# Softmax division moved from the probabilities to the result of P V, in the attention blocks of a hybrid decoder kernel

## The chip, the cores and the metric

The kernel runs on one core of one Trainium2 chip. It is measured in device microseconds (us) from start to end of one execution; less is better. The core has a matrix engine (PE, with its weight loads as PEld), a vector engine (DVE), a scalar engine (ACT), GpSimd (POOL) and a queue engine (SP). Each runs its own list of instructions in order and waits for the others by semaphores. PE writes to PSUM, which is cut into banks; DVE and ACT read PSUM and the on-chip memory SBUF.

## What is computed

The reference is a decoder trunk of two layers over 512 tokens of width 1024, in float32. Each layer has three mixers side by side (sparse attention, a diagonal state space "S5", a chunked state space "SSD"), an output projection, and an MLP of width 4096. Only the attention matters here, cut to its core:

```python
def attend(args):                              # one block of 128 queries
    ...
    _, sel = lax.top_k(score, topk)            # 128 keys for each query
    ...
    logits = jnp.where(valid[:, :, None, None, :], logits, -jnp.inf)
    p = jax.nn.softmax(logits, axis=-1).astype(v_sel.dtype)
    o = jnp.einsum('bqgrk,bqkgd->bqgrd', p, v_sel)
    return o.reshape(b, Q_BLOCK, ATTN_WIDTH)
```

There are 8 heads of width 64: 2 key/value groups g with 4 heads r each. There are 4 query blocks per layer.

## The kernel before

Each layer is written as several streams of work (projections, index scores, top-k, attention, S5, SSD, output projection), as Python generators that `merge` steps in turn by the costs that they yield (`pace`, `start`); the instructions then get their places on each engine from a priority list (`prio`) and from when buffers come free. So a change in one stream also shifts where the instructions of others stand. PSUM has two pools of four banks, "m" and "a"; the plan of each layer says which pool a tile comes from.

`attend` handles one query block b, with (b + 1) x 128 keys. For each group g and head r: PE makes the logits `lg` (L1033, in `head_dot`), DVE applies the top-k mask and takes the row's extreme in one pass (L1085, tile `pe`), and ACT does exp in place, with the row sum into `sm` (L1086; the tile's name in the trace is `psum`). After the four heads of a group, DVE takes the reciprocal of the sums (L1089). Then the four tiles of probabilities are multiplied by it: head 0 on ACT (L1093, from the plan's `norm_act`), heads 1 to 3 on DVE (L1095). For each 128 keys, PE transposes the four tiles of a group (L1101, tile `pTp`), ACT copies them to SBUF (L1103, `pT`), and PE multiplies with the values (L1106, `po`; group 0 to PSUM partitions 0 to 63, group 1 to 64 to 127). At the end each of four 128x128 slices of `po` is split in a high part `mh` (ACT, L1110) and a low part `ml` (DVE, L1111), which feed the output projection (`pm`, L436 to L438, result added to x by DVE at L1341).

Work that stands between, on the same engines: top-k (MAX and MATCH_REPLACE, L1064 and L1065, DVE), the SSD mixer (`cv`, `CT` L836, `dec` L874 on DVE; `arow`, `ssds` L871, `ssdy` L885 and L887, `st` on PE), the S5 mixer (`X` L714 on DVE; `s5y`, `glu` on PE), and the split of the next block's queries (`hhl` L1021 on DVE, then `hTp` on PE).

Of the kernel before, what the change touches and what calls it, by code (L numbers as in the profile page):

```python
# [10 lines left out]
F32 = mybir.dt.float32  # L11
F32R = mybir.dt.float32r
I32 = mybir.dt.int32
AF = mybir.ActivationFunctionType
ALU = mybir.AluOpType
# [3 lines left out]
P = 128  # L19
# [26 lines left out]
    "top": ((1, 2, 3),),  # L46
    "out": (("att",), ("s5", "ssd")),
    "serial": "no",
    "norm_act": (),
    "tab_dve": (),  # L50
    "pace": {"w": 1.0, "key": 1.0, "idx": 1.0, "top": 1.0, "q": 1.0, "att": 1.0, "s5": 1.0, "ssd": 1.0, "out": 1.0,
             "tab": 1.0},
    "start": {"tab": 0.0, "key": 0.0, "top": 0.0, "att": 0.0, "s5": 0.0, "ssd": 0.0, "out": 0.0},
    "prio": {},
# [3 lines left out]
}  # L58
# [3 lines left out]
        "top": ((2, 1), (3,)),  # L62
        "out": (("s5",), ("att",), ("ssd",)),
        "serial": "no",
        "norm_act": (0,),
        "tab_dve": ("B1", "C2"),
        "pace": {"w": 0.29, "key": 2.007, "idx": 0.686, "top": 0.061, "q": 3.616, "att": 1.702, "s5": 0.084, "ssd": 2.496, "out": 1.504, "tab": 0.3},
        "start": {"tab": 0.5, "key": 5.0, "top": 41.0, "att": 0.0, "s5": 12.0, "ssd": -7.0, "out": 20.0},
        "prio": {"att": 300, "idx": -30, "top": -300, "ssd": 300, "tab": -30, "w": 30, "s5": 30, "out": -30, "q": -300},
        "bank": {"w_kv": "m", "w_qi": "m", "w_q": "m", "w_u5": "m", "w_xa": "a", "w_xb": "m", "w_z": "m", "kT": "a", "hT": "a", "ix": "a", "lg": "a", "pT": "m", "po": "a", "sB": "m", "sst": "a", "sU": "a", "sv": "m", "sy": "m", "st": "m", "sg": "a", "dds": "a", "dseg": "m", "darow": "m", "dT": "a", "ds": "a", "dy": "a", "dst": "a", "dn": "a", "db": "m"},  # L70
    },
    {
        "w_order": ("kv", "xa", "qi", "z", "u5", "q", "xb"),
        "top": ((1,), (2,), (3,)),
        "out": (("s5",), ("att",), ("ssd",)),
        "serial": "no",
        "norm_act": (0,),
        "tab_dve": (),
        "pace": {"w": 0.344, "key": 1.011, "idx": 1.036, "top": 0.873, "q": 3.741, "att": 1.652, "s5": 0.357, "ssd": 1.82, "out": 0.453, "tab": 0.853},
        "start": {"tab": 0.0, "key": 0.0, "top": 15.0, "att": -20.0, "s5": -30.0, "ssd": 3.0, "out": 22.0},  # L80
        "prio": {"tab": -30, "out": -100, "att": 1000, "q": -300, "idx": -30, "s5": 1000, "top": -100},
        "bank": {"w_kv": "m", "w_qi": "m", "w_q": "m", "w_u5": "m", "w_xa": "a", "w_xb": "m", "w_z": "m", "kT": "a", "hT": "a", "ix": "b", "lg": "a", "pT": "a", "po": "a", "sB": "m", "sst": "a", "sU": "m", "sv": "m", "sy": "a", "st": "b", "sg": "a", "dds": "a", "dseg": "m", "darow": "m", "dT": "m", "ds": "m", "dy": "a", "dst": "a", "dn": "a", "db": "m"},
    },
)
WB = (3, 5)
# [115 lines left out]
class Net:  # L201
# [868 lines left out]
    def attend(self, b, qT, K, mask, nrs, ah, al):  # L1070

        nc = self.nc
        v = nc.vector
        nk = (b + 1) * P
        po = self.ps(self.bank["po"], (P, 4, P), name="po")
        es = []
        for g_ in range(2):
            sm = self.s([P, 4], tag="psum", bufs=4)
            for r in range(4):
                p = self.ps(self.bank["lg"], name="lg")[:, :nk]  # L1080
                self.head_dot(p, qT[2 * r + g_], K, g_, nk)
                e = self.g(name="pe")[:, :nk]
                nm = self.s([P, 1], tag="nmax", bufs=8)
                h = 2 * r + g_
                v.tensor_tensor_reduce(e, p, mask, nrs[:, h:h + 1], 3.0e38, ALU.add, ALU.min, nm)  # L1085
                nc.scalar.activation(e, e, AF.Exp, bias=nm, scale=-1.0, accum_out=sm[:, r:r + 1])  # L1086
                es.append(e)
                yield self.pace["att"] * (0.4 + 0.25 * b)
            v.reciprocal(sm, sm)  # L1089
            for r in range(4):  # L1090
                e = es[4 * g_ + r]
                if r in self.plan["norm_act"]:
                    nc.scalar.activation(e, e, AF.Copy, scale=sm[:, r:r + 1])  # L1093
                else:
                    v.tensor_scalar(e, e, sm[:, r:r + 1], None, ALU.mult)  # L1095
        for kb in range(b + 1):
            pts = []
            for g_ in range(2):
                p = self.ps(self.bank["pT"], (P, 4, P), name="pTp")
                for r in range(4):  # L1100
                    nc.tensor.transpose(p[:, r], es[4 * g_ + r][:, kb * P:(kb + 1) * P], self.ident)  # L1101
                pt = self.g([P, 4, P], name="pT")
                nc.scalar.activation(pt, p, AF.Copy)  # L1103
                pts.append(pt)
            for g_ in range(2):
                nc.tensor.matmul(po[g_ * 64:g_ * 64 + 64], self.vt[:, kb, g_], pts[g_], start=kb == 0, stop=kb == b)  # L1106
            yield self.pace["att"] * 2.2
        bs = slice(b * P, (b + 1) * P)
        for r in range(4):
            nc.scalar.activation(ah[r][:, bs], po[:, r], AF.Copy)  # L1110
            v.tensor_tensor(al[r][:, bs], po[:, r], ah[r][:, bs].bitcast(F32), ALU.subtract)  # L1111


    def merge(self, name, streams):
# [409 lines left out]
```

## Time and profile before

| | us |
|---|---|
| median of 3 runs | 1334.06 (1333.53 to 1334.45) |
| the profiled execution, its own time | 1331.74 |
| its span, first to last instruction | 1330.0 |
| PE busy in the span | 1219.8 (92%) |
| DVE busy | 884.2 (66%) |
| ACT busy | 554.9 (42%) |

The granted clock of PE is 0.962 of full on average over the span. In the trace's rows, a start is in us from the span's first instruction, then comes the time that the row spans, the engine, the line, what is written from what, the shape, the number of records, and in brackets the idle time of that engine just before with what ended it. A matmul in full float32 leaves two records.

### The profile page before, as it was taken

Reading aid. Unit: us, or ns where it says so; the run is one execution under the profiler, and the core shown is the slowest. Engines: PE = TensorE matmul, PEld = TensorE weight load, DVE = VectorE, ACT = ScalarE, POOL = GpSimd, SP = SyncE. Lnnn points to the kernel's source line nnn. Section 1 sums busy time; section 2 is a strip of 40 time slices with the busy share of each in tenths; the row PEclk is TensorE's granted clock in tenths of the full one; section 3 lists DMA queues with packets and bytes.
Section 4 is the critical chain, followed back from the end, with each engine's and each line's share of the span. In section 5 each row is a group of like instructions: output and inputs, shape, how many; then the busy total and the mean of one; then the engine's idle time right before and its main releaser. Section 6 shows DMA issues by size and latency. Waiting matters only on the chain. (4 is left out here: it accounts for less than half of the span.)

```text
span 1330.0 us, 16738 instructions
## 1 busy us (share of the span) xinstructions
PE 1219.8 (92%) x5708; PEld 979.4 (74%) x5708; DVE 884.2 (66%) x2024; ACT 554.9 (42%) x1128; POOL 167.1 (13%) x302
## 2 busy tenths in 40 slices
PE   5678967889999999999999978967999999999998
PEld 5657755458888877888887867744788888888886
DVE  7998999857865444454575899996575445444443
ACT  4345543664532432423445535655354233242331
POOL 2494100000696030000000000000000000000000
PEclk9789978899999999999999989978999999999999
DMA  6122220002333323333323332100133333333332
GB/s 197 48 72 64 73 81 22 11 1 71 95 97 103 95 62 118 97 96 96 97 79 82 102 83 58 47 9 17 51 93 95 98 100 96 96 96 99 99 111 80
DMA packets 107430, 105.83 MB, mean 80 GB/s; under 512 B 15184, under 2 KB 99920, under 8 KB 107344
## 3 DMA queue, kind: packets, MB, share of 16 engines
q1 hardware_dynamic: 107344, 104.76, 26.5%
q8 instruction: 45, 0.74, 0.2%
q14 instruction: 41, 0.34, 0.1%
HBM read 100.41 MB, written 3.15 MB: 78 GB/s over the span
## 5 line engine op out<-in xcount | busy, mean ns | idle before, releaser
L172 DVE TENSOR_TENSOR wlo<-wraw,whi 128x512 fp32r<-128x512 f32 (+1 forms) x368 | 260.5, 710 | 285.0 <-ACT whi L171 284.1
L171 ACT ACTIVATE whi<-wraw 128x512 fp32r<-128x512 f32 (+1 forms) x368 | 229.1, 624 | 487.0 <-PE pm L437 343.1
L436 PE MATMUL pm<-xh,whi 128*128 128x512 f32 x640 | 252.4, 395 | 3.9 <-ACT q L1199 3.9
L437 PE MATMUL pm<-xl,whi 128*128 128x512 f32 x640 | 251.5, 393 | 0.0
L438 PE MATMUL pm<-xh,wlo 128*128 128x512 f32 x640 | 250.7, 392 | 0.0
L438 PE MATMUL pm<-uh,wlo 128*128 128x512 f32 x512 | 199.3, 390 | 1.2 <-DVE wlo L172 1.2
L437 PE MATMUL pm<-ul,whi 128*128 128x512 f32 x512 | 199.4, 390 | 0.0
L436 PE MATMUL pm<-uh,whi 128*128 128x512 f32 x512 | 199.4, 389 | 0.0
L436 PEld LDWEIGHTS pm<-xh,whi 128*128 128x128 f32 x640 | 121.0, 189 | 30.5 <-ACT q L1199 4.6
L438 PEld LDWEIGHTS pm<-xh,wlo 128*128 128x128 f32 x640 | 121.1, 189 | 25.4 <-DVE wlo L172 0.2
L437 PEld LDWEIGHTS pm<-xl,whi 128*128 128x128 f32 x640 | 121.1, 189 | 24.4 <-issue 0.2
L438 PEld LDWEIGHTS pm<-uh,wlo 128*128 128x128 f32 x512 | 96.1, 188 | 21.7 <-DVE wlo L172 1.6
L437 PEld LDWEIGHTS pm<-ul,whi 128*128 128x128 f32 x512 | 96.1, 188 | 20.3 <-issue 0.4
L436 PEld LDWEIGHTS pm<-uh,whi 128*128 128x128 f32 x512 | 96.1, 188 | 20.0 <-issue 0.2
L436 PE MATMUL pm<-whi,xh 128*128 128x512 f32 (+1 forms) x176 | 67.8, 388 | 13.8 <-ACT xh L372 11.7
L437 PE MATMUL pm<-wlo,xh 128*128 128x512 f32 (+1 forms) x176 | 66.8, 380 | 4.9 <-DVE wlo L172 4.9
L438 PE MATMUL pm<-whi,xl 128*128 128x512 f32 (+1 forms) x176 | 66.4, 382 | 2.2 <-DVE xl L374 2.2
L1376 DVE TENSOR_TENSOR ul<-ur,uh 128x512 fp32r<-128x512 f32 x64 | 48.4, 757 | 22.5 <-ACT uh L1375 22.4
L1374 DVE SCALAR_TENSOR_TENSOR ur<-pm,ur 128x512 f32<-128x512 f32 x64 | 43.9, 686 | 24.4 <-ACT ur L1371 24.4
L1382 DVE TENSOR_TENSOR sq<-pm,r2b 128x512 f32<-128x512 f32 x64 | 44.2, 690 | 23.1 <-PE pm L438 23.1
L1375 ACT ACTIVATE uh<-ur 128x512 fp32r<-128x512 f32 x64 | 40.0, 625 | 32.4 <-DVE ur L1374 32.4
L436 PE MATMUL pm<-mh,whi 128*128 128x512 f32 x128 | 51.4, 403 | 0.7 <-DVE x L1341 0.7
(343 smaller groups left out, 1859.3 us busy)
## 6 DMA issues: line engine op xcount, KB each, us to landing
wraw<-in_w_up_dram SPq DMA_DIRECT2D x128, 256.0 KB, 2.7
wraw<-in_w_down_dram SPq DMA_DIRECT2D x128, 256.0 KB, 2.7
wraw<-in_w_in_dram SPq DMA_DIRECT2D x64, 256.0 KB, 2.8
wraw<-in_w_out_dram SPq DMA_DIRECT2D x32, 256.0 KB, 2.7
wraw<-in_w_in_dram SPq DMA_DIRECT2D x16, 166.0 KB, 2.3
x<-in_xT_dram SPq DMA_DIRECT2D x8, 256.0 KB, 5.6
out_dram<-x SPq DMA_DIRECT2D x8, 256.0 KB, 2.1
s5bc<-in_s5bc_dram SPq DMA_DIRECT2D x4, 256.0 KB, 4.4
```

Source lines behind the costliest of these rows:

```text
L171: nc.scalar.activation(hi, raw, AF.Copy)
L172: nc.vector.tensor_tensor(lo, raw, hi.bitcast(F32), ALU.subtract)
L436: nc.tensor.matmul(p, lh, rh, start=first, stop=False)
L437: nc.tensor.matmul(p, lh, rl, start=False, stop=False)
L438: nc.tensor.matmul(p, ll, rh, start=False, stop=last)
L1374: v.scalar_tensor_tensor(r, p, 0.0, r, ALU.max, ALU.mult)
L1375: nc.scalar.activation(h, r, AF.Copy)
L1376: v.tensor_tensor(lo, r, h.bitcast(F32), ALU.subtract)
L1382: v.tensor_tensor(t, d[1], rb, ALU.mult)
```

## The change

The probabilities stay undivided. `sm` now holds the sums of both groups, and one reciprocal of 128x8 follows the last exp of the block. Eight small matmuls (`rsb`, after L1091) take a column of reciprocals, repeated to 64 columns, as the stationary operand and the identity as the moving one. This puts the reciprocals of a head along the free axis and the same row on 64 partitions, in the layout of `po`. ACT copies the bank to SBUF (`rn`, after L1093). After P V, DVE multiplies `po` by `rn` in one 128x512 pass (after L1107), and `mh` and `ml` are made from `rn` in SBUF. The scalings and the plan's `norm_act` are gone. `rsb` takes a bank of pool "m" in layer 0 and of "a" in layer 1. For the code around it, a line of the kernel after is the line of before less 3 ahead of the reciprocal, and less 1 to 3 behind it.

```diff
         es = []
+        sm = self.s([P, 2, 4], tag="psum", bufs=2)
         for g_ in range(2):
-            sm = self.s([P, 4], tag="psum", bufs=4)
             for r in range(4):
...
-                nc.scalar.activation(e, e, AF.Exp, bias=nm, scale=-1.0, accum_out=sm[:, r:r + 1])
+                nc.scalar.activation(e, e, AF.Exp, bias=nm, scale=-1.0, accum_out=sm[:, g_, r:r + 1])
                 es.append(e)
                 yield self.pace["att"] * (0.4 + 0.25 * b)
-            v.reciprocal(sm, sm)
-            for r in range(4):
-                e = es[4 * g_ + r]
-                if r in self.plan["norm_act"]:
-                    nc.scalar.activation(e, e, AF.Copy, scale=sm[:, r:r + 1])
-                else:
-                    v.tensor_scalar(e, e, sm[:, r:r + 1], None, ALU.mult)
+        v.reciprocal(sm, sm)
+
+        p = self.ps(self.bank["rsb"], (P, 4, P), name="rsb")
+        for r in range(4):
+            for g_ in range(2):
+                nc.tensor.matmul(p[g_ * 64:g_ * 64 + 64, r], sm[:, g_, r:r + 1].to_broadcast([P, 64]), self.ident, start=True, stop=True)
+        rn = self.g([P, 4, P], name="rn")
+        nc.scalar.activation(rn, p, AF.Copy)
         for kb in range(b + 1):
...
+        v.tensor_tensor(rn, po, rn, ALU.mult)
         for r in range(4):
-            nc.scalar.activation(ah[r][:, bs], po[:, r], AF.Copy)
-            v.tensor_tensor(al[r][:, bs], po[:, r], ah[r][:, bs].bitcast(F32), ALU.subtract)
+            nc.scalar.activation(ah[r][:, bs], rn[:, r], AF.Copy)
+            v.tensor_tensor(al[r][:, bs], rn[:, r], ah[r][:, bs].bitcast(F32), ALU.subtract)
```

Over the whole program PE gets 64 matmuls more, DVE goes from 1882 to 1834 instructions and ACT from 1044 to 1036. The change also moves others.

PE in layer 0, block 2, before, from the last logits: the first four transposes are followed by the first P V matmul of group 0 alone, then by `ssdy`, and group 1's transposes come after that.

```order
L1033 MATMUL lg_2731<-kl_767,hT_2626 128x384
L1101 MATMUL pTp_2743<-cons,pe_2661 128x128
...
L1106 MATMUL po_2656<-pT_2748,vt_119 64x512
L885 MATMUL ssdy_2775<-dec_2650,xd_2690 64x128
L887 MATMUL ssdy_2775<-cs_2728,prev_2637 64x128
...
L1101 MATMUL pTp_2750<-cons,pe_2704 128x128
```

The same place after, from the same logits:

```order
L1030 MATMUL lg_2729<-kl_767,hT_2630 128x384
L1091 MATMUL rsb_2737<-cons,psum_2661 64x128 x8
L1099 MATMUL pTp_2748<-cons,pe_2665 128x128
...
L1099 MATMUL pTp_2755<-cons,pe_2702 128x128
...
L1104 MATMUL po_2660<-pT_2753,vt_119 64x512
L1104 MATMUL po_2660<-pT_2760,vt_119 64x512
```

`rsb` stands ahead of all transposes of the block, the two P V matmuls of the first 128 keys now stand side by side, and `ssdy` has moved behind them. Blocks 1 to 3 of both layers are alike in this.

DVE in layer 1, block 1, before, at the end of the block: the four `ml` alternate with the convolution `cv` of the SSD mixer.

```order
L1185 TENSOR_TENSOR xb_8284<-pm_8206,rb_6952 128x512
L1064 MAX mx_2157_8781<-isc_7331 128x8
L822 TENSOR_SCALAR cv_8308<-xb_8284,hconvw,hconvb 128x512
L1111 TENSOR_TENSOR ml_7967<-po_8115,mh_7963 128x128
L825 SCALAR_TENSOR_TENSOR cv_8308<-xb_8284,hconvw,cv_8308 128x511
L1111 TENSOR_TENSOR ml_7968<-po_8115,mh_7964 128x128
L825 SCALAR_TENSOR_TENSOR cv_8308<-xb_8284,hconvw,cv_8308 128x510
```

The same place after:

```order
L1184 TENSOR_TENSOR xb_8295<-pm_8217,rb_6960 128x512
L1107 TENSOR_TENSOR rn_8193<-po_8125,rn_8193 128x512
L819 TENSOR_SCALAR cv_8319<-xb_8295,hconvw,hconvb 128x512
L1110 TENSOR_TENSOR ml_7975<-rn_8193,mh_7971 128x128
...
L822 SCALAR_TENSOR_TENSOR cv_8319<-xb_8295,hconvw,cv_8319 128x511
L1340 TENSOR_TENSOR x_107<-x_107,pm_8385 128x512
L822 SCALAR_TENSOR_TENSOR cv_8319<-xb_8295,hconvw,cv_8319 128x510
```

The multiplication by `rn` now waits for `po` ahead of the whole convolution, and all four `ml` stand ahead of its later taps. From here to the first `CT` of this stretch, three MAX and three MATCH_REPLACE follow, where one and two followed before.

## Rows read from the trace of the kernel before

**Rows 1.** The page, part 1: busy us, share of the span, instructions.

```profile
PE   1219.8 (92%) x5708; PEld 979.4 (74%) x5708; DVE 884.2 (66%) x2024; ACT 554.9 (42%) x1128; POOL 167.1 (13%) x302
```

**Rows 2.** Stretches of the span: length, PE busy (records), granted clock, DMA share, GB/s.

```profile
200.00:300.00 100.00, 80.61 (x387) 0.90 0.03 11
840.00:940.00 100.00, 78.80 (x402) 0.90 0.07 22
940.00:1320.00 380.00, 380.00 (x1700) 1.00 0.31 96
```

**Rows 3.** PE in order of time: start, us, line, operation, records.

```profile
249.36 0.66 PE L885 MATMUL ssdy<-dec,xd 128*64 128x128 f32 x8
263.32 1.07 PE L1106 MATMUL po<-pT,vt 128*64 128x512 f32 x2
264.80 1.08 PE L1106 MATMUL po<-pT,vt 128*64 128x512 f32 x4
...
344.13 1.05 PE L408 MATMUL bct<-cons,r 128*128 128x128 f32 x8
```

**Rows 4.** Groups by line, whole program: busy us, mean ns | idle before.

```profile
L1341 DVE TENSOR_TENSOR x<-x,pm 128x512 f32<-128x512 f32 x48 | 32.1, 682 | 8.8 <-PE pm L438 8.4
L1103 ACT ACTIVATE pT<-pTp 128x512 f32<-128x512 f32 x40 | 22.7, 598 | 26.1 <-PE pTp L1101 26.1
L1095 DVE TENSOR_SCALAR pe<-pe,psum 128x128 f32<-128x128 f32 (+3 forms) x48 | 15.7, 383 | 0.1
```

**Rows 5.** PE in order of time, layer 0, blocks 1, 2 and 3.

```profile
235.74 0.97 PE L1101 MATMUL pTp<-cons,pe 128*128 128x128 f32 x4 [1.80 <-ACT pe L1093]
237.70 1.97 PE L1106 MATMUL po<-pT,vt 128*64 128x512 f32 x2 [0.99 <-ACT pT L1103]
...
256.04 0.96 PE L1101 MATMUL pTp<-cons,pe 128*128 128x128 f32 x4 [0.48 <-ACT pe L1093]
257.72 1.07 PE L1106 MATMUL po<-pT,vt 128*64 128x512 f32 x2 [0.72 <-ACT pT L1103]
...
260.47 1.71 PE L1101 MATMUL pTp<-cons,pe 128*128 128x128 f32 x12 [0.81 <-ACT pe L1093]
...
280.00 0.66 PE L1101 MATMUL pTp<-cons,pe 128*128 128x128 f32 x4 [0.80 <-ACT pe L1093]
282.54 1.07 PE L1106 MATMUL po<-pT,vt 128*64 128x512 f32 x2 [1.88 <-ACT pT L1103]
```

**Rows 6.** ACT in order of time: the last exp of blocks 1 and 2, layer 0.

```profile
236.58 0.49 ACT L1086 ACTIVATE pe<-pe,nmax 128x256 f32<-128x256 f32 x1
...
258.79 0.61 ACT L1086 ACTIVATE pe<-pe,nmax 128x384 f32<-128x384 f32 x1 [1.12 <-DVE nmax L1085]
```

**Rows 7.** Stretches, columns as in rows 2: PE after two waits of rows 5.

```profile
235.70:242.40 6.70, 5.67 (x18) 0.53 0.13 40
...
284.00:288.00 4.00, 4.00 (x17) 0.58 0.00 0
```

**Rows 8.** Layer 1 in order of time, one row of DVE, then PE.

```profile
871.03 0.29 DVE L1111 TENSOR_TENSOR ml<-po,mh 128x128 fp32r<-128x128 f32 x1 [1.88 <-ACT mh L1110]
```

**Rows 9.** PE in order of time, layer 1.

```profile
881.56 0.80 PE L871 MATMUL ssds<-CT,cv 128*128 128x128 f32 x2 [5.84 <-DVE CT L836]
...
897.12 0.44 PE L1101 MATMUL pTp<-cons,pe 128*128 128x128 f32 x2 [1.34 <-ACT pe L1093]
...
917.83 0.45 PE L885 MATMUL ssdy<-dec,xd 128*64 128x128 f32 x4 [4.23 <-DVE dec L874]
```

**Rows 10.** Layer 0, S5 and block 0, in order of time: DVE, then PE.

```profile
189.28 0.68 DVE L1095 TENSOR_SCALAR pe<-pe,psum 128x128 f32<-128x128 f32 x3
```

**Rows 11.** PE, layer 0, S5 and block 0.

```profile
190.60 0.47 PE L727 MATMUL s5y<-CA,X 128*64 128x128 f32 x1 [3.36 <-DVE X L714]
...
213.25 2.45 PE L1106 MATMUL po<-pT,vt 128*64 128x512 f32 x4 [6.02 <-ACT pT L1103]
```

More of the change, by code (lines that the diff above doesn't have):

```diff
@@ L48 @@
     "serial": "no",
-    "norm_act": (),
     "tab_dve": (),
@@ L64 @@
         "serial": "no",
-        "norm_act": (0,),
         "tab_dve": ("B1", "C2"),
@@ L69 @@
         "prio": {"att": 300, "idx": -30, "top": -300, "ssd": 300, "tab": -30, "w": 30, "s5": 30, "out": -30, "q": -300},
-        "bank": {"w_kv": "m", "w_qi": "m", "w_q": "m", "w_u5": "m", "w_xa": "a", "w_xb": "m", "w_z": "m", "kT": "a", "hT": "a", "ix": "a", "lg": "a", "pT": "m", "po": "a", "sB": "m", "sst": "a", "sU": "a", "sv": "m", "sy": "m", "st": "m", "sg": "a", "dds": "a", "dseg": "m", "darow": "m", "dT": "a", "ds": "a", "dy": "a", "dst": "a", "dn": "a", "db": "m"},
+        "bank": {"w_kv": "m", "w_qi": "m", "w_q": "m", "w_u5": "m", "w_xa": "a", "w_xb": "m", "w_z": "m", "kT": "a", "hT": "a", "ix": "a", "lg": "a", "pT": "m", "po": "a", "rsb": "m", "sB": "m", "sst": "a", "sU": "a", "sv": "m", "sy": "m", "st": "m", "sg": "a", "dds": "a", "dseg": "m", "darow": "m", "dT": "a", "ds": "a", "dy": "a", "dst": "a", "dn": "a", "db": "m"},
     },
@@ L76 @@
         "serial": "no",
-        "norm_act": (0,),
         "tab_dve": (),
@@ L81 @@
         "prio": {"tab": -30, "out": -100, "att": 1000, "q": -300, "idx": -30, "s5": 1000, "top": -100},
-        "bank": {"w_kv": "m", "w_qi": "m", "w_q": "m", "w_u5": "m", "w_xa": "a", "w_xb": "m", "w_z": "m", "kT": "a", "hT": "a", "ix": "b", "lg": "a", "pT": "a", "po": "a", "sB": "m", "sst": "a", "sU": "m", "sv": "m", "sy": "a", "st": "b", "sg": "a", "dds": "a", "dseg": "m", "darow": "m", "dT": "m", "ds": "m", "dy": "a", "dst": "a", "dn": "a", "db": "m"},
+        "bank": {"w_kv": "m", "w_qi": "m", "w_q": "m", "w_u5": "m", "w_xa": "a", "w_xb": "m", "w_z": "m", "kT": "a", "hT": "a", "ix": "b", "lg": "a", "pT": "a", "po": "a", "rsb": "a", "sB": "m", "sst": "a", "sU": "m", "sv": "m", "sy": "a", "st": "b", "sg": "a", "dds": "a", "dseg": "m", "darow": "m", "dT": "m", "ds": "m", "dy": "a", "dst": "a", "dn": "a", "db": "m"},
     },
```

2 rows, old and new, of the table _PLAN are left out of this document.

## The prediction

> **What bounds the kernel now.** First the page's busy times: PE is busy 92% of the span, DVE 66% [rows 1]. An average over stages hides where either of them waits, so the stretches come next [rows 2]. From 940 us to the end PE is busy all the time: there a delay that reaches PE is simply added to the end, and a gain taken off. In the two attention stretches, 200 to 300 and 840 to 940 us, PE is busy only 80.6 and 78.8 of 100 us, and at 0.90 of its clock. The whole change lies in these stretches and shortly ahead of the first. So the question is only when PE gets through the eight attention blocks (four in each layer).
>
> Then the waits of PE inside a block, in order of time [rows 5]. In layer 0 PE stands idle for the scaled probabilities (ACT `pe` L1093) and for the copy of the transposes (ACT `pT`): 1.80 and 0.99 us in block 1; 0.48, 0.72 and 0.81 in block 2; 0.80 and 1.88 in block 3. The scaling is what ends these waits, but not what fills them: the second group's exps are still running on ACT meanwhile. In layer 1 the largest waits are for DVE: 5.84 us for `CT`, 4.23 us for `dec` [rows 9].
>
> Last the clock [rows 7]: behind the waits of block 1 PE ran 6.7 us at 0.53 of its clock, behind those of block 3 4.0 us at 0.58. Half clock is 1.2 GHz in place of 2.4. So a wait costs more than itself.
>
> **The price of what is added.** *The broadcast matmuls.* The trace of before has no `rsb`. Two rows bound it. The `bct` matmuls have the same form (a repeated column against the identity) but fill all 128 output rows: 8 records in 1.05 us [rows 3]; the last one's latency is in that, and 16 records take about twice as much, near 1.8 to 1.9 us. The `ssdy` matmuls have 64 output columns and alternate between the lower and upper 64 partitions, as `rsb` does: 8 records in 0.66 us, which with the last one's 0.27 or so of latency taken off leaves 0.055 us a record, or 0.9 us for the 16 records of a block. I take 0.9 us at full clock, since shape and alternation are those of `ssdy`; at half clock twice that, 1.8. P V shows the same: two records of one group alone span 1.07 us, four records of both groups side by side 1.08 [rows 3].
>
> The Trainium skill (TensorE: Matmul & The Clock Gate, Part 3: Packing small matmuls) says that narrow matmuls whose outputs lie in different column groups run at the same time. The `ssdy` and P V rows agree. By that rule `rsb` costs 8 x 0.9 = 7 us over the program, without it 14; the sum below goes by the rows.
>
> *The copy and the multiplication.* The ACT copy `rn` is like the `pT` copy, 0.60 us; the DVE pass over 128x512 with one operand in PSUM is like `x`, 0.68 us [rows 4]. The copy lies ahead of the block's first `pT` on ACT, but beside PE's transposes. The multiplication is bare at the block's end: `mh`, `ml` and what stands behind them on DVE wait for it, where before they read `po` at once.
>
> **What is removed.** 48 scalings on DVE of 0.383 us, 15.7 us in all [rows 4], and 16 on ACT. Less eight multiplications of 0.68 (5.5 us), DVE has 10 us less to do. This counts only where PE waits for DVE.
>
> **What is moved.** `rsb` stands in order ahead of all transposes of its block, and it needs all eight sums. So PE now waits once per block for the last exp, where it waited twice or three times for shares of it and did the first group's transposes in between. In exchange the two P V matmuls of the first 128 keys stand side by side in six blocks. Alone they cost 1.0 each, together between 1.0 and 1.5: 0.5 us gained per block, 1 at best.
>
> **The sum, block by block.**
> Layer 0, ahead of block 0: three scalings (0.68 us) and a reciprocal go from in front of `X` [rows 10], which PE waits 3.36 us for [rows 11]; the same happened once more for the first group. I take -1.3.
> Block 0: `rsb` stands ahead of `glu` where four transposes stood, +0.5; the second four transposes need the bank that `rsb` holds until ACT's copy, which stands behind S5's `mh` on ACT, so P V (now at 213.25, after 6.02 us of waiting [rows 11]) starts some 0.7 later. +1.2.
> Block 1: the last exp ends at 236.58 + 0.49 less the scaling of 0.5 that stood between on ACT, so near 236.7 [rows 6]; with the reciprocal `rsb` starts near 237.0. PE's last logits end at 235.74 - 1.80 = 233.94. Idle 3.1 in place of 2.79: +0.3. `rsb` at half clock +1.8, the pair at half clock -0.9. The multiplication stands ahead of `ml` and of the second `hhl`, for which PE waits: +0.6. Together +1.8.
> Block 2: the last exp starts at 258.79 because DVE's three scalings (1.1 us) stand ahead of its mask pass [rows 6]; it will start near 257.8 and end at 258.4. The reciprocal stands behind a MAX: `rsb` near 258.9. PE is idle from 255.56 (256.04 - 0.48): 3.3 us in one piece in place of 2.01 in three, +1.3. The 12 records of `ssdy` that kept PE going between stand behind P V now. The waits in pieces left the clock full; a wait of 1.80 us in one piece, in block 1, was followed by half clock. So I count a new stretch of half clock: 4 to 6.7 us at about half cost 2 to 3 us [rows 7]; +2.9 with `rsb`'s 0.9 in it. The pair -0.5, `hhl` +0.6. Together +4.3, without the drop of the clock +2.3.
> Block 3: idle near 2.5 in place of 0.80 + 1.88, -0.2; `rsb` +0.9; one pair more -0.5; at the end the output projection waits for the multiplication and `mh`, and the last `ssdy` for a `dec` that stands behind it on DVE: +1.0. Together +1.2.
> Layer 0: -1.3 + 1.2 + 1.8 + 4.3 + 1.2 = +7.2.
>
> Layer 1, block 0: dense matmuls around it hide the waits, so `rsb` itself: +0.9. Block 1: `CT`, for which PE waits 5.84 us [rows 9], comes later. Between the end of P V and `CT` stand, more than before, the multiplication, one step of `cv`, two MAX and one MATCH_REPLACE: five passes over 128x512, by the `x` row 3.4 us. Less 1.2, as the pair ends 0.5 earlier, and DVE starts at once rather than after a first `mh`, which it waited for as part of 1.88 us [rows 8]: +2.2, of which 0.7 comes back, since that top-k work is then missing later. Block 2: the wait of 1.34 goes [rows 9], `rsb`, the wait for `pT` and `hhl` come: 0. Block 3: three scalings go from in front of `dec`, so 1.2 off the 4.23 [rows 9]; `rsb` at half clock +1.8, the pair -0.9, the end +0.5: +0.2. Layer 1: 0.9 + 1.5 + 0 + 0.2 = +2.6.
>
> Together +9.8; I take +9 as the pairs may give more than I counted. On the profiled execution, 1331.74 us, this gives 1340.7. Its own time lies 2.3 below the median of the runs, so against the median, 1334.06, the forecast is **1343 us**.
>
> **The rivals.**
> *Dearer waits, some 1350 us.* If `rsb` runs one by one as `bct` does, 8 x 0.9 = 7 more; or if the clock also falls in block 2 of layer 1, +2 to 3, and stays low longer where it fell. For it: half clock lasted 6.7 us in block 1. Against it: the `ssdy` row.
> The same page of the Trainium skill (Loop structure matters more than you think) asks to keep matmuls back to back, since a wait between bursts lets the clock fall. It speaks against one long wait per block. The trace agrees in block 1, not in block 2, where short waits left the clock full.
> *Faster, some 1329 us.* DVE sets the pace in layer 1: PE's waits for `CT` and `dec` are 10 us [rows 9]. Three blocks' scalings stand ahead of the second, 18 x 0.383 = 6.9 us, less three multiplications, 2.0. If that 4.9 arrives at `dec` whole and block 2 of layer 0 keeps its clock with full pairs (-2.9 - 2), then +9 becomes about -5: the layer 1 terms +2.6 turn into -4, layer 0's +7.2 into about 0 or -1. It decides whether `CT` lands ahead of 881.56 or behind. Against it: the order of DVE, which puts more ahead of `CT`.
> *No change, 1331.4 to 1336.7 us.* `rsb` falls into the idle time that is there anyway and the clock holds in block 2: layer 0 near +3, layer 1 near 0, and the pairs gain another 2 us: +1.
> That the scalings are not really gone can be left out, since the order of DVE no longer has them.
>
> **Chances.** Forecast (1337 to 1347) 0.47, dearer 0.17, no change 0.19, faster 0.17. A difference below 0.2% (2.7 us) can't be told from none in a measurement of this kernel; so faster 0.17, same 0.19, slower 0.64. The range 1330 to 1350 leaves out half of the dearer case and the better half of the faster one, near 0.17.
>
> **What would show it.** In the trace after: `rsb` x16 in 0.9 or 1.8 us at full clock; PE idle ahead of `rsb` near 3 us in blocks 1 and 2 of layer 0; granted clock near 0.5 from 259 us; P V's first four records in 1.0 to 1.5; `CT` of layer 1 about 2 us later against its block's logits. The prediction is wrong if PE's idle sum in 200 to 300 and 840 to 940 shrinks, or if the clock holds behind the single waits.

## The result, and the profile after

The changed kernel takes 1340.59 us (median; 1338.08 to 1341.48), the kernel before, beside it, 1334.06: a ratio of 1.0054 [1.0043, 1.0064]. It is slower by 0.5%, 6.5 us. Its profiled execution took 1340.0 us with a span of 1338.2, at a mean granted clock of 0.959 of full. Against the profiled execution of before the span is 8.2 us longer.

First the page of after, part 1 (busy us, share of the span, instructions), and the stretches, to be read against [rows 1, 2]:

```profile
PE 1226.1 (92%) x5836; PEld 989.0 (74%) x5836; DVE 871.9 (65%) x1976; ACT 551.2 (41%) x1120; POOL 167.6 (13%) x302
```

```profile
200.00:300.00 100.00, 78.67 (x407) 0.86 0.04 11
...
840.00:940.00 100.00, 78.95 (x448) 0.88 0.07 22
940.00:1320.00 380.00, 379.75 (x1709) 1.00 0.31 95
```

DVE has 12.3 us less to do, as the scalings are gone (its records go from 2024 to 1976, the same 48 fewer as in the order of instructions). What their going from in front of S5 bought, 3.4 us ahead of block 0 by the table below, is more than lost again: in 200 to 300 us PE is busy 2 us less than before although it has more to do there, and its clock is 0.86 in place of 0.90. From 940 us on PE is still full, so what is lost ahead of it stays lost.

Next PE of after in order of time, to be read against [rows 5]. Columns: start, us, engine, line, operation, records, and in brackets the idle time ahead with what ended it.

```profile
234.79 1.98 PE L1091 MATMUL rsb<-cons,psum 128*64 128x128 f32 x16 [3.05 <-DVE psum L1086]
236.70 2.39 PE L1099 MATMUL pTp<-cons,pe 128*128 128x128 f32 x10
239.02 1.41 PE L1104 MATMUL po<-pT,vt 128*64 128x512 f32 x4
...
246.85 0.66 PE L1021 MATMUL hTp<-cons,hhl 128*128 128x128 f32 x4 [1.98 <-DVE hhl L1018]
...
256.87 1.98 PE L1091 MATMUL rsb<-cons,psum 128*64 128x128 f32 x16 [3.25 <-DVE psum L1086]
258.77 2.18 PE L1099 MATMUL pTp<-cons,pe 128*128 128x128 f32 x9
260.89 2.30 PE L1104 MATMUL po<-pT,vt 128*64 128x512 f32 x4
...
273.16 1.09 PE L1021 MATMUL hTp<-cons,hhl 128*128 128x128 f32 x4 [1.72 <-DVE hhl L1018]
...
285.50 1.09 PE L1091 MATMUL rsb<-cons,psum 128*64 128x128 f32 x16 [2.85 <-DVE psum L1086]
286.52 1.80 PE L1099 MATMUL pTp<-cons,pe 128*128 128x128 f32 x8
```

In blocks 1 to 3 of layer 0 there is now one wait of about 3 us, and it is for the reciprocal (DVE `psum`). In block 2, where the waits were 0.48, 0.72 and 0.81 us and the clock stayed full, `rsb` now runs in 1.98 us, and the transposes and P V behind it at half clock too (four P V records in 2.30 us; 1.08 at full clock [rows 3]).

How far after lags behind before, at the same instruction of each (start times of PE, after less before, us), tells where the 8.2 us come in. These are two single executions, and their distance is 1.7 us more than that of the medians, so a step of about 1 us in the table needn't be there in every execution:

| place | lag | gained (-) or lost since |
|---|---|---|
| layer 0, `s5yT` of S5, ahead of block 0 | -3.39 | -3.39 |
| end of block 0's P V | -1.54 | +1.85 |
| first logits of block 1 | -2.25 | -0.71 |
| end of block 1's P V | -2.56 | -0.31 |
| second `hTp` behind it | -1.92 | +0.64 |
| end of block 2's P V | +1.72 | +3.64 |
| second `hTp` behind it | +2.30 | +0.58 |
| last logits of block 3 | +3.45 | +1.15 |
| `bct`, behind the output projection | +4.71 | +1.26 |
| layer 1, first `hTp` | +5.76 | +1.05 |
| first logits of block 1 | +6.12 | +0.36 |
| `CT` arrives | +8.29 | +2.17 |
| first `ssdy` behind the last `dec` | +8.91 | +0.62 |
| `bct` of layer 1 | +8.21 | -0.70 |

### The profile page after: what moved, and what is told of

It reads as the page before. It is cut to its first block, busy times and chain, and to the rows that moved or that the text cites. A ratio compares the mean times of both kernels' runs of the same rounds, so it can differ in the third digit from the quotient of the medians.

```text
span 1338.2 us, 16947 instructions
## 1 busy us (share of the span) xinstructions
PE 1226.1 (92%) x5836; PEld 989.0 (74%) x5836; DVE 871.9 (65%) x1976; ACT 551.2 (41%) x1120; POOL 167.6 (13%) x302
## 4 chain that ended last, share of the span: by engine, by line
PE 73%; DVE 17%; ACT 4%; issue 3%; DMA 2%; POOL 1%; SPq 0%; ACTq 0%; DVEq 0%
PE pm L433 21%; PE pm L434 21%; PE pm L435 21%; PE po L1104 2%; DVE wlo L169 2%; PE pTp L1099 2%; DVE isc L1062 1%; DVE mx L1061 1%; DVE isc L1051 1%; DVE pe L1082 1%; ACT pe L1083 1%; DMA wraw<-in_w_in_dram 1%; PE rsb L1091 1%; DVE cv L822 1%; PE hTp L1021 1%
## 5 line engine op out<-in xcount | busy, mean ns | idle before, releaser
L433 PE MATMUL pm<-whi,xh 128*128 128x512 f32 (+1 forms) x176 | 68.9, 394 | 14.5 <-ACT xh L369 12.3
L1062 DVE MATCH_REPLACE8 isc<-mx,isc 128x256 f32<-128x256 f32 (+2 forms) x96 | 51.6, 540 | 0.0
```

The lines of the kernel that those rows point to most:

```text
L433: nc.tensor.matmul(p, lh, rh, start=first, stop=False)
L1062: v.match_replace(acc, m8, acc, SENT)
```

## The experiments

Two theories stood at the start. **Theory 1, the place:** the cost is not in the added operations but in where the broadcast stands, ahead of all transposes, so that PE waits once, long, and its clock falls. **Theory 2, the operations:** broadcast, copy and multiplication cost what they take, wherever they stand. A third point was how far the multiplication at the block's end counts (theory A: little; theory B: most).

### Without any division

```diff
-        p = self.ps(self.bank["rsb"], (P, 4, P), name="rsb")
...
-        nc.scalar.activation(rn, p, AF.Copy)
...
-        v.tensor_tensor(rn, po, rn, ALU.mult)
...
-            nc.scalar.activation(ah[r][:, bs], rn[:, r], AF.Copy)
+            nc.scalar.activation(ah[r][:, bs], po[:, r], AF.Copy)
...
```

The kernel after without broadcast, copy and multiplication; `mh` and `ml` read `po` again. It leaves out the division.

> The kernel after without rsb, rn and the multiplication: mh and ml are made from po as in the kernel before. The division by the sums is left out. This is the most that taking the scalings away can give. Theory 1 and 2: S5's gain of 3.4 us stays, and the waits of PE for the scaled probabilities (in layer 0 1.80, 0.48, 0.81 and 0.80 us, in layer 1 some 5) shrink: 1322 to 1328 us, so the broadcast and the multiplication together cost 12 to 18 us in the kernel after. Rival (DVE's relief is worth nothing outside S5): 1329 to 1332 us.

Measured: 1305.42 us (1304.09 to 1306.78), ratio 0.9791 [0.9778, 0.9804]. That is far below what was expected. So dividing costs 29 us of the kernel before and 35 us of the kernel after: much more was to be had than the prediction's sum, which only weighed one place of the division against the other.

### Broadcast or multiplication

Two kernels split those 35 us. One keeps the broadcast and leaves out the multiplication:

```diff
-        v.tensor_tensor(rn, po, rn, ALU.mult)
...
-            nc.scalar.activation(ah[r][:, bs], rn[:, r], AF.Copy)
+            nc.scalar.activation(ah[r][:, bs], po[:, r], AF.Copy)
...
```

> The kernel after without the multiplication behind P V: mh and ml read po, as before. rsb and its copy stay, with nobody to read the copy; so the division is left out. PE's order in the attention blocks is that of the kernel after. What it gains against after is the price of the tail. Theory A (most of the 35 us between the kernel after and the one with neither broadcast nor multiplication, 1305.4, is the place of rsb): the tail is some 0.6 to 1 us per block and 2 at CT of layer 1, so 7 to 9 us: 1331 to 1334 us. Theory B (most is the tail): 1318 to 1325 us.

Measured: 1335.30 us (1332.95 to 1337.23), 5.3 under after; ratio to before 1.0012 [1.0002, 1.0023].

The other keeps the multiplication, by a tile that lies ready, and leaves out the reciprocal, the broadcast and the copy:

```diff
-        v.reciprocal(sm, sm)
-        p = self.ps(self.bank["rsb"], (P, 4, P), name="rsb")
...
-        nc.scalar.activation(rn, p, AF.Copy)
...
-        v.tensor_tensor(rn, po, rn, ALU.mult)
+        v.tensor_tensor(rn, po, self.vt.rearrange(...), ALU.mult)
```

> The kernel after without the broadcast matmuls and their copy: the multiplication behind P V stays, but by another 128x512 tile that lies in SBUF, so the division is left out. The transposes then stand between the logits, as in the kernel with neither. Against that one, 1305.4 us, it shows the tail alone. Theory A: 1312 to 1315 us. Theory B (the tail is most of it): 1320 to 1328 us. The broadcast alone is what is left up to the kernel with rsb behind the first transposes, 1324.2.

Measured: 1311.33 us (1307.66 to 1315.86), ratio 0.9834 [0.9809, 0.986]. Both agree: the multiplication at the end of a block is worth 5 to 6 us (1340.6 - 1335.3; 1311.3 - 1305.4), the broadcast in its place 29 us (1340.6 - 1311.3; the runs of the second kernel spread over 8 us). Both times lie about 1 us outside what theory A expected (1331 to 1334, and 1312 to 1315), and far from theory B (1318 to 1325, and 1320 to 1328): theory A holds. And 29 us is more than the broadcast takes: `rsb` is 12.1 us of PE in the whole program. As an estimate, that leaves 17 us for its place.

### The same broadcast, one step later

The broadcast and the copy are written behind the transposes of the first 128 keys, ahead of P V. Nothing else in the code changes.

```diff
-        p = self.ps(self.bank["rsb"], (P, 4, P), name="rsb")
...
-        nc.scalar.activation(rn, p, AF.Copy)
         for kb in range(b + 1):
...
                 pts.append(pt)
+            if kb == 0:
+                p = self.ps(self.bank["rsb"], (P, 4, P), name="rsb")
...
+                nc.scalar.activation(rn, p, AF.Copy)
             for g_ in range(2):
```

> The kernel after, with the eight rsb matmuls and the copy rn issued behind the transposes of the first 128 keys instead of ahead of them; all else as after. In PE's order of blocks 1 and 2 of layer 0 the transposes then stand between and right behind the logits, and rsb just ahead of P V. Theory 1 (the place: PE waits once per block for all eight sums before it may transpose, and the clock falls behind that wait): the term of block 2 in layer 0, +3.7 us, goes almost whole, and some 1 us each in block 1 and 3 of layer 0 and block 2 of layer 1: 1334 to 1336 us, and the granted clock in the 10 us around block 2's P V above 0.95. Theory 2 (the cost: 8 x 1 to 1.9 us of extra matmuls on a full PE): rsb is as long as before, so 1339 to 1341 us. Theory 3 (the tail: the multiplication at the block's end): unchanged, 1339 to 1341 us.

Measured: 1324.23 us (1322.67 to 1327.7), ratio 0.9936 [0.9922, 0.995]. That is 16 us under after, and 9 under before; theory 1 expected the sign, but with 5 to 7 us under after well under half the size. PE in order of time in blocks 1 and 2 of this kernel:

```profile
233.56 0.33 PE L1092 MATMUL pTp<-cons,pe 128*128 128x128 f32 x1 [0.17 <-ACT pe L1083]
234.05 0.33 PE L1092 MATMUL pTp<-cons,pe 128*128 128x128 f32 x1 [0.16 <-ACT pe L1083]
234.54 0.33 PE L1092 MATMUL pTp<-cons,pe 128*128 128x128 f32 x1 [0.17 <-ACT pe L1083]
234.80 1.97 PE L1100 MATMUL rsb<-cons,psum 128*64 128x128 f32 x16
...
255.16 1.07 PE L1104 MATMUL po<-pT,vt 128*64 128x512 f32 x2 [0.15 <-ACT pT L1094]
256.43 0.33 PE L1092 MATMUL pTp<-cons,pe 128*128 128x128 f32 x1 [0.21 <-ACT pe L1083]
...
256.74 0.32 PE L1100 MATMUL rsb<-cons,psum 128*64 128x128 f32 x1
256.90 0.99 PE L1100 MATMUL rsb<-cons,psum 128*64 128x128 f32 x14
```

`rsb` starts when it did in after (234.80 and 256.74 against 234.79 and 256.87): the sums are not ready earlier. But by then PE has done the transposes, one by one as each exp ended, and in block 2 also P V of the first group. The wait is no longer idle. The groups by line (busy us, mean ns | idle ahead of them, and what ended it) give the sum over the program, first after, then this kernel:

```profile
L1091 PE MATMUL rsb<-cons,psum 128*64 128x128 f32 x128 | 12.1, 348 | 15.3 <-DVE psum L1086 11.9 <-DVE ge L741 3.4
L1099 PE MATMUL pTp<-cons,pe 128*128 128x128 f32 x160 | 27.2, 321 | 6.0 <-ACT rn L1093 5.9
```

```profile
L1092 PE MATMUL pTp<-cons,pe 128*128 128x128 f32 x160 | 29.0, 287 | 8.6 <-ACT pe L1083 4.7 <-DVE ge L741 3.4
L1100 PE MATMUL rsb<-cons,psum 128*64 128x128 f32 x128 | 11.4, 332 | 5.9 <-ACT pT L1094 5.9
```

The 3.4 behind `ge` and the 5.9 in block 0 stand in both. What differs is 11.9 us of waiting for the reciprocal, in place of which there are 4.7 us for single exps: 7.2 less. In 200 to 300 us PE is then busy 84.01 us at a clock of 0.91 (0.86 in after), in 840 to 940 us 83.51 at 0.90 (0.88). As an estimate, 0.05 and 0.02 of 100 us each at the clock are another 7 us, and the two together come near the 16. The expectation had counted the waits and little of the clock. The sum is rough, and that it comes so near is in part luck: by start times, the profiled execution of this kernel gains 7.1 us on that of after up to `bct` of layer 0 (341.74 against 348.84), 2.8 between the layers, where it is the clock (see below), and 6.5 in layer 1.

### The broadcast last

Here broadcast and copy stand behind all P V of the block, ahead of the multiplication alone.

```diff
-        p = self.ps(self.bank["rsb"], (P, 4, P), name="rsb")
...
-        nc.scalar.activation(rn, p, AF.Copy)
         for kb in range(b + 1):
...
         bs = slice(b * P, (b + 1) * P)
+        p = self.ps(self.bank["rsb"], (P, 4, P), name="rsb")
...
+        nc.scalar.activation(rn, p, AF.Copy)
         v.tensor_tensor(rn, po, rn, ALU.mult)
```

> The changed kernel with its broadcast (eight small matmuls and the copy of 512 columns) written behind all P V matmuls of a block, ahead of the multiplication alone. The transposes then stand between the logits, as in e_mid, and TensorE waits for no sum ahead of P V. At the end of a block the path gets the broadcast (1.09 us at full clock, 1.98 at half), the copy (0.60) and two hand-overs (0.2 each): 2.1 to 3.0 a block, less what the next step's queued matmuls hide. Theory 1 (what made the change dear is that every transpose and P V stood behind the last sum): at or a little above e_mid's 1324, 1321 to 1331. Theory 2 (the cost is the broadcast's own time and its copy, wherever they stand, and e_mid was hiding them behind the first exponentials): back by 8 x 2.1 = 17 us towards the changed kernel, 1335 to 1345.

Measured: 1323.71 us (1323.04 to 1324.46), ratio 0.9925 [0.9911, 0.9939]: the same as one step later, although the copy and its hand-overs now stand bare ahead of the multiplication. As the cause of what the place costs, theory 2 falls. A part stays, wherever the broadcast stands: out of the way of the transposes it still costs 12 to 13 us over the kernel without it (1323.7 and 1324.2 against 1311.3). That is near the 11.4 to 12.2 us that `rsb` takes on PE, but that PE's time is what this part consists of is argued, not shown; further down, 5.7 us more of `rsb` leave the end where it was.

### One wait, with the old scalings

Does one wait for all sums cost as much without the broadcast? The kernel before with its scalings held back until all eight exps have been issued:

```diff
+        sm = self.s([P, 2, 4], tag="psum", bufs=2)
...
-            v.reciprocal(sm, sm)
+        v.reciprocal(sm, sm)
+        for g_ in range(2):
             for r in range(4):
                 e = es[4 * g_ + r]
...
```

> The kernel before, with its scalings of the probabilities kept, but one reciprocal of 128x8 behind all eight exps and the scalings of both groups behind that: the one wait of the change without its broadcast matmuls, its copy and its multiplication. Theory 1 (the one wait and the clock): slower than before, since the wait is even longer by the scalings, with half clock behind it in blocks 1 to 3 of layer 0: 1339 to 1343 us. Theory 2 (the cost of the matmuls) and theory 3 (the multiplication at the end): none of it is here, so within 2 us of before, 1332 to 1336 us.

Measured: 1333.24 us, ratio 0.9996 [0.9988, 1.0005]. In the total theory 1's expectation failed, and the time is the one that the other theories gave; but the trace shows that this is two effects of about the same size, and not none. PE of this kernel in order of time:

```profile
193.84 1.09 PE L738 MATMUL s5yT<-cons,ysb 128*128 128x128 f32 x8 [0.48 <-ACT ysb L731]
...
234.96 2.61 PE L1102 MATMUL pTp<-cons,pe 128*128 128x128 f32 x9 [3.79 <-ACT pe L1094]
...
256.58 2.48 PE L1102 MATMUL pTp<-cons,pe 128*128 128x128 f32 x9 [3.89 <-ACT pe L1094]
```

The waits are in one piece, with half clock behind them, as theory 1 has it. From `s5yT` to `bct` layer 0 loses 3.9 us against before. But `s5yT` itself comes 2.7 us earlier (193.84; 196.56 before), since the scalings no longer stand in front of `X`. So that gain belongs to moving the scalings and not to the broadcast, and one wait, here with the scalings at its end, costs some 4 us in layer 0. After's blocks lose 8.1 there (from -3.4 to +4.7).

### Work in the gap

If block 2 is dear because the clock falls in the long wait, then matmuls of no use in that wait should make the kernel faster. Sixteen of them, on the probabilities of the sixth and seventh head, in block 2 of layer 0 alone, into the bank that `rsb` then overwrites:

```diff
+        if b == 2 and self.bank["rsb"] == "m":
+            for i in range(16):
+                nc.tensor.matmul(p[:, i % 4], self.ident, es[5 + i // 8][:, :P], start=True, stop=True)
```

> The kernel after, and in block 2 of layer 0 sixteen matmuls without use ahead of rsb, on the probabilities of the sixth and seventh head, into the bank that rsb then overwrites: PE has work in the last part of the one wait of 3.25 us that stood there. If the half clock behind that wait is what made this block dear: rsb at 1.0 in place of 1.9 us, the ten transposes behind it 1.1 in place of 2.2, and the time 2 to 3 us lower, 1337.5 to 1338.6. If the clock is nothing to the time, or falls anyway: 1340 to 1342, the more so as the added work may delay rsb.

Measured: 1335.04 us (1330.93 to 1336.92), ratio 1.0011 [0.9999, 1.0022], 5.5 under after. PE of this kernel in order of time, then two stretches of after and the same two of this kernel (length, PE busy, granted clock, DMA share, GB/s):

```profile
253.54 3.84 PE L1091 MATMUL rsb<-pe,cons 128*128 128x128 f32 x32 [0.58 <-ACT pe L1083]
257.31 1.09 PE L1094 MATMUL rsb<-cons,psum 128*64 128x128 f32 x16
258.33 1.31 PE L1102 MATMUL pTp<-cons,pe 128*128 128x128 f32 x10
259.68 1.56 PE L1107 MATMUL po<-pT,vt 128*64 128x512 f32 x4
...
271.11 0.63 PE L1021 MATMUL hTp<-cons,hhl 128*128 128x128 f32 x4 [1.73 <-DVE hhl L1018]
```

```profile
250.00:260.00 10.00, 6.47 (x38) 0.80 0.01 2
260.00:270.00 10.00, 9.81 (x51) 0.86 0.00 0
```

```profile
250.00:260.00 10.00, 9.12 (x71) 1.00 0.01 2
260.00:270.00 10.00, 9.19 (x56) 1.00 0.00 0
```

The first row is the filling: 3.84 us, and `rsb` starts 0.4 later than in after. The clock then stays at 1.00, and `rsb` takes 1.09 us in place of 1.98. This kernel came 0.7 us earlier into the block; at the second `hTp` it is 2.05 ahead (271.11 against 273.16), and that `hTp` and the logits behind it run at full clock, so at block 3's `rsb` it is 3.2 ahead (282.28 against 285.50). Up to there blocks 2 and 3 thus gain 2.5 us, as expected. The rest of the 5.5 lies where nothing was changed and isn't accounted for by the filling: the 0.7 stands already at `s5yT`, ahead of block 0, another 0.7 comes in between the layers, and 1.1 in layer 1. The Trainium skill (TensorE: Matmul & The Clock Gate, Loop structure matters more than you think) says that matmuls stay at speed when the loops keep them back to back; this run shows it in one place, with work that is thrown away.

### All of one half, then all of the other

Does `rsb` gain from alternating between the lower and upper 64 rows?

```diff
-        for r in range(4):
-            for g_ in range(2):
+        for g_ in range(2):
+            for r in range(4):
```

> The kernel after, with the loops over group and head of rsb exchanged: four matmuls to the lower 64 partitions, then four to the upper, in place of alternating. Same work, same place. If neighbours to different halves run at the same time, as the ssdy rows of the kernel before showed, the 16 records take 1.8 to 1.9 us at full clock in place of 1.0, and at half clock 3.6 in place of 1.9. Theory 2 (PE's time in rsb goes to the end one to one): 8 x 0.85 us and more at half clock, so 1347 to 1351 us. Theory 1 (the wait counts, not the matmuls): the waits in front do not change and rsb is on the path behind them just the same, so also 1346 to 1350. Rival: no pairing in rsb, or hidden: 1340 to 1342 us.

Measured: 1339.90 us (1338.25 to 1340.41), ratio 1.0046 [1.0034, 1.0058], within 1 us of after. The group of `rsb` in this kernel, to set beside after's 12.1 above:

```profile
L1091 PE MATMUL rsb<-cons,psum 128*64 128x128 f32 x128 | 17.8, 355 | 15.6 <-DVE psum L1086 12.2 <-DVE ge L741 3.4
```

And block 1 of it on PE in order of time, to set beside after's rows at 234.79 and 236.70:

```profile
233.65 2.88 PE L1091 MATMUL rsb<-cons,psum 128*64 128x128 f32 x16 [3.05 <-DVE psum L1086]
236.46 1.60 PE L1099 MATMUL pTp<-cons,pe 128*128 128x128 f32 x10
```

Four and four takes half as long again: 17.8 in place of 12.1 us. At the end next to nothing is seen of these 5.7, where both theories had expected 1346 us or more; only the rival (hidden) comes near. In block 1 `rsb` takes 0.9 more, but the ten records behind it take 1.60 in place of 2.39, as the clock is back sooner. That this is why the end stays is argued from this place, and not shown for the other blocks.

### The multiplication in four slices

With the place settled, the multiplication was cut into four slices of 128 columns, each ahead of its `mh`, in both kernels with a moved broadcast.

```diff
-        v.tensor_tensor(rn, po, rn, ALU.mult)
         for r in range(4):
+            v.tensor_tensor(rn[:, r], po[:, r], rn[:, r], ALU.mult)
```

Broadcast ahead of the first P V:

> The kernel with rsb behind the first transposes (1324.2 us), with the multiplication cut into four slices of 128x128, each just ahead of its mh and ml. On DVE four times 0.285 in place of 0.69 us, 0.45 more per block; but the first mh starts 0.4 us earlier. If the output projection's first matmuls at the end of block 3 are what waits: 0.4 us gained in each layer, some 1 us in all, 1322.5 to 1324. If what stands behind all of it on DVE waits (hhl of the next block, CT in layer 1): 0.45 us lost in six blocks, 1325 to 1327.

Measured: 1323.13 us (1318.1 to 1323.78), ratio 0.9911 [0.989, 0.9932]: the fastest of the kernels that divide, but its distance from the one with a whole multiplication is 1 us, inside the spread of the runs.

Broadcast last:

> e_late with the multiplication cut into four slices of 128 columns, each ahead of its mh copy, so that the first mh starts after 0.28 us of multiplication instead of 0.69. Theory 1 and 2 alike: 0.4 us a block at most, 0 to 3 us under e_late. Against e_midsplit's 1323.1 it tells which place is better when all else is equal: theory 1 expects the two within 4 us of each other, theory 2 expects this one 12 us or more above.

Measured: 1329.57 us (1328.6 to 1331.02), ratio 0.9969 [0.9958, 0.9981]: 5.9 slower than with a whole multiplication, where 0 to 3 faster was expected. Against the sliced kernel with the broadcast ahead of P V it is 6.4 slower, more than the 4 of theory 1 and half of the 12 of theory 2, so this pair doesn't tell which place is better. At the start of layer 1 it is only 0.8 behind, at `CT` 0.7. Then come these stretches, first of the kernel with a whole multiplication, then of this one:

```profile
876.00:880.00 4.00, 3.79 (x16) 0.50 0.01 2
880.00:884.00 4.00, 3.56 (x27) 0.87 0.00 0
884.00:888.00 4.00, 3.90 (x26) 1.00 0.01 4
```

```profile
876.00:880.00 4.00, 3.17 (x14) 0.50 0.00 0
880.00:884.00 4.00, 3.27 (x16) 0.50 0.00 2
884.00:888.00 4.00, 4.00 (x20) 0.50 0.00 0
```

Behind the wait for `CT` both run at half clock. In the first the clock is back near 881 us, in the second only near 891, and block 2's logits take twice as long there. PE was somewhat less busy ahead of it (3.17 and 3.27 of 4 us, not 3.79 and 3.56). That this kept the clock down was not tried by itself. So 0.7 us at `CT` had become 5.9 us by `bct` (955.78 against 949.86).

## Why the prediction was right, and where its steps were off

The forecast was 1343 (1330 to 1350), slower; measured were 1340.6, slower by more than 0.2%. Its sum was +9.8, taken as +9, on the profiled execution; the trace has +8.2. The step from the profiled execution to the median added 2.3 us that are not there: the profiled run of after lies 0.6 below its median, that of before 2.3 below. The prediction's own sign of being wrong, less idle time of PE, did not come: in 200 to 300 and 840 to 940 us PE idles 42.4 us, 40.6 before.

Layer 0 came to +4.7 in place of +7.2, layer 1 to +2.4 in place of +2.6, and +1.1 fell between them. The direction and the two dear places, block 2 of layer 0 and `CT` of layer 1, came by the steps named. That the sum is so near is in part luck: S5 and block 1 came out 2.1 and 1.5 us better than forecast, block 3 and the stretch between the layers 1.2 and 1.1 worse.

- **S5, mis-sized.** -1.3 was taken, -3.4 measured, as both of PE's waits for `X` moved, and the first one, too, had a group's reciprocal and scalings in front of it: on DVE `X` came 2.2 us earlier at the first and 3.2 at the second. Three scalings and a reciprocal are some 0.7 us each time, which is the 1.3 of the sum; the rest is other work of DVE that moved behind `X` (before the second one stood, with the scalings, an `isc` pass of 0.64 us at 188.64, which follows `X` now), and the sum had no term for it. The run with one wait and the old scalings shows the same gain (-2.7) without any broadcast.
- **Block 0.** +1.2 predicted, +1.9 measured; the cause is the one named, the bank: the second four transposes wait for the copy `rn`, 5.94 us. Then 0.7 comes back in dense work, which was not foreseen: behind block 0 the clock is full again at 215.1 us, before it was at 218.9.
- **Block 1.** The wait is right (3.1 predicted, 3.05), `rsb` at half clock is right (1.8; 1.9 to the next start). Without the +0.6 for `hhl` +1.2 was predicted, -0.3 measured. What the sum lacked is that the clock comes back sooner: it is near 0.5 from 234.8 to 239.0 us and full behind that, where before it was 0.53 for 6.7 us [rows 7]. So the four P V records in 1.41 us ran at full clock and the two of before, in 1.97, at half; at half clock four take 2.30 (block 2). What the pair alone is worth can't be read from these rows. The +0.6 for `hhl` is right in both blocks (+0.64, +0.58).
- **Block 2, right.** +3.7 without `hhl` was predicted, +3.6 measured, by the steps that the prediction names: 3.25 us of idle time in one piece (3.3), and half clock from there (0.80 in 250 to 260 us, 1.00 before). The filled gap shows the clock to be the cause of most of it: with the clock kept up, 2.5 us go.
- **Block 3.** The wait of 2.85 is near the 2.5. But the clock fell once more, ahead of the block, behind the wait of 1.72 us for `hhl`: +1.2, not in the sum. From the last logits on, +1.3 is near the forecast +1.2.
- **Between the layers** +1.1 came in behind S5 of layer 1, and it is the clock. PE waits 2.90 us for `q` in both kernels, and then the same 31 matmuls stand ahead of the first `hTp`; they take 8.77 us before and 9.92 after, as half clock lasts from 830.0 to 833.5 us before, and from within the wait to 839.7 after (rows below). In the kernel with the broadcast one step later the same 31, behind a wait of 2.91 us, run at full clock in 7.18 us. The change does not touch this code; why these matmuls ran 0, 3.4 or 5.9 us at half clock behind the same wait stays open.
- **Layer 1.** `CT` is +2.5 later against block 1's P V (+2.2), and 0.4 comes back (0.7). Block 2 was put at 0 and lost 1.1, as the clock fell there, near 905 us: the dearer rival's second mechanism, in small. Block 3 gave 0.7 back where +0.2 was forecast. PE's wait for `dec` is 2.23 us, down from 4.23, but not because `dec` came sooner, as the forecast had it: it lags 8.9 us, as much as the end of block 2's P V. PE came later, with a wait of 1.70 us for `hhl` (0.89 before) and half clock behind it.

The stretch between the layers, before and then after: its clock (columns as in [rows 2]) and the first matmul behind the wait.

```profile
820.00:845.00 25.00, 20.98 (x94) 0.93 0.20 63
829.16 0.50 PE L436 MATMUL pm<-xh,whi 128*128 128x512 f32 x1 [2.90 <-ACT q L1199]
```

```profile
820.00:845.00 25.00, 22.10 (x90) 0.86 0.11 32
833.77 0.79 PE L433 MATMUL pm<-xh,whi 128*128 128x512 f32 x1 [2.90 <-ACT q L1198]
```

The rows of after for the `CT` step and for `dec`, to be read against [rows 9] (PE), then DVE ahead of `CT`:

```profile
889.85 0.79 PE L868 MATMUL ssds<-CT,cv 128*128 128x128 f32 x2 [5.83 <-DVE CT L833]
...
926.74 0.45 PE L882 MATMUL ssdy<-dec,xd 128*64 128x128 f32 x4 [2.23 <-DVE dec L871]
```

```profile
876.49 0.69 DVE L1107 TENSOR_TENSOR rn<-po,rn 128x512 f32<-128x512 f32 x1 [1.34 <-PE po L1104]
877.10 0.54 DVE L819 TENSOR_SCALAR cv<-xb,hconvw,hconvb 128x512 f32<-128x512 f32 x1
877.56 0.90 DVE L1110 TENSOR_TENSOR ml<-rn,mh 128x128 fp32r<-128x128 f32 x4
878.38 0.74 DVE L822 SCALAR_TENSOR_TENSOR cv<-xb,hconvw,cv 128x511 f32<-128x511 f32 x1
```

DVE idles 1.34 us for the end of P V, and only then can the convolution go on.

**What the prediction did not ask.** The rival "faster, some 1329" was given 0.17 and its mechanism put down to DVE. Its price does not follow from its terms: +9 less 4.9 less 4.9 is near -1, not -5, so they give some 1333 and not 1329. With the broadcast one step later something of that kind is seen: layer 1 gains 4.1 us against before (from a lead of 4.2 at its first `hTp` to 8.3 at its `bct`), 3.0 of it between `CT` and `dec` (33.3 us apart, 36.3 before, 36.9 after). That DVE's shorter list is the cause is likely but not shown. The shorter wait for `dec`, 2.56 us in place of 4.23, does not show it, as the kernel with one wait, which keeps all scalings, waits 2.55. In the kernel after nothing of this gain is left. The prediction took that place as given; it priced the one wait, and in block 2 rightly, but the same change with the broadcast behind the transposes, or behind all P V, is 9 to 10 us faster than before.

## What to carry to other kernels

Taking the softmax division out of the probabilities paid here only where nothing of the division stood ahead of the work that no longer needs it: the same change came to +6.5 us with its eight matmuls in front of the transposes, and to -9 and -10 with them behind the transposes and behind P V. On an engine that takes its instructions in order, write a step where its result is wanted, not where its inputs are complete, and look in the order for what queues behind it. And count a long wait in one piece as dearer than its length, because the clock of PE may fall behind it: in block 2 three waits of 0.48, 0.72 and 0.81 us left it full, one of 3.25 us was followed by half clock. How long it then stays down differed even in the same code, so where that decides, price both states.

## What the runs showed of the hardware

Matmuls with 64 output rows that alternate between the two halves overlap: 16 records of `rsb` took 1.02 us to the next start at full clock, and over the program 12.1 us against 17.8 with four and four. The Trainium skill (TensorE: Matmul & The Clock Gate, Part 3: Packing small matmuls) says that small matmuls in different tiles of the array run at the same time; the trace agrees, with a gain of 1.5 times (17.8 / 12.1) from two halves.

With 16 matmuls whose results are thrown away a kernel was 5.5 us faster; 2.5 of it lies in the two blocks where they kept the clock up, the rest is not explained by them. Behind the same wait of 2.9 us, and in the same 31 matmuls, PE ran 3.4 us at half clock before, 5.9 after, and none in the kernel with the broadcast one step later. And two kernels that were less than 1 us apart at a wait of 5.8 to 6.0 us left it with the clock back after some 5 us in one and some 14 in the other (881 and 891 us).
